# 512-column products in the gate and in the output projection's second half of a two-layer encoder trunk, with their low weights at six offsets

## The chip, the core and the metric

The kernel runs on one core of a Trainium2 chip. Its time is the device time of one execution in microseconds, lower is better; medians are over several executions.

## What is computed

Two layers work on a sequence of 256 positions with 2048 channels, all in float32.

```
h = x
for each layer:
    hn = rmsnorm(h);  u = hn @ w_in            # 5632 columns: conv value, conv gate, z, q, k, v, z2
    ya = swish(layernorm(conv31(value * sigmoid(gate)))) * silu(z)
    yb = window_attention(q, k, v) * silu(z2)
    h  = h + concat(ya, yb) @ w_out            # 2048 x 2048, the output projection
    e  = rmsnorm(p @ w_pe)
    h  = h + e * sigmoid(h @ w_pg)             # 2048 x 2048, the gate
return rmsnorm(h)
```

## The kernel before

Everything is kept transposed: channels on the 128 partitions, the 256 positions along the free dimension. A tile of 128 output channels is a sum over 16 slices of 128 input channels.

**Products.** The products are made in a reduced form of float32 (f32r), three for each slice. Both operands are split into a high part (rounded to f32r) and a low part (the rest): high weights with high operand, high weights with low operand, low weights with high operand. `mm3` (lines 398 to 403) issues these three products of 256 columns, and each brings its own load of 128x128 weights, so the high weights are loaded twice:

```
L401  matmul(o, w[:, 0], x[:, 0], ...)      # high weights, high operand
L402  matmul(o, w[:, 0], x[:, 1], ...)      # high weights, low operand
L403  matmul(o, w[:, 1], x[:, 0], ...)      # low weights, high operand
```

**Weights.** They come as a stream of *halves*: 128x1024 numbers each, 8 slices of one output tile. There are 156 per layer in a fixed order (`weight_halves`), the output projection's first half (the channels of `yb`) at 92 to 107, its second half (those of `ya`) at 108 to 123, the gate at 124 to 155. Two halves are one DMA of 1024 KB from SyncE (`load`). `split` makes a half's high part by a cast on ScalarE (line 168) and its low part by a subtraction on VectorE (line 171). `get` runs the splits four halves ahead of the products; five buffers (`NSPL`) hold split halves, so half n+5 can be cast only when TensorE is done with half n. `SHIFT` places both parts 16 numbers (64 bytes) into their buffer, the low part right behind the high one.

**Order.** The queues of TensorE, VectorE and ScalarE run in the order in which the program writes them (`MAN`). An instruction that waits holds up everything behind it on its engine. After each half `pump` lets side work go on by a step: in the gate the normalised embedding's products (line 540), one instruction per half, and in the projection the low part of the residual of the pair before (line 771).

**Output projection.** First for all 16 tiles the slices of `yb`, then (lines 761 to 775) for all 16 the slices of `ya`: a pair of tiles shares one PSUM bank, one VectorE add of 128x512 puts it on the residual (line 769), a cast on ScalarE makes the residual's high part (line 770), a subtraction its low part (line 771). High and low part of the residual, `h1`, are the gate's operand.

**Gate.** Pairs of tiles again, two halves for each tile. `gate(j, b)` (lines 785 to 811) adds the residual's two parts (line 790), takes the sigmoid of the PSUM bank on ScalarE (line 792), multiplies and adds on VectorE (lines 794, 795) and squares for the next norm on ScalarE (line 391 or 800), with the accumulation on GpSimd. In the last layer two ScalarE copies scale the result for the output (line 808). The last two tiles go one by one. The first pair takes the lower eight slices of both tiles, then the upper eight.

At the border of the layers the sum of squares (`rstd_col`, line 354) needs the square of the gate's last tile.

Of the kernel before, what the change touches and what calls it, by code (L numbers as in the profile page):

```python
# [10 lines left out]
F32 = mybir.dt.float32  # L11
# [6 lines left out]
P = 128  # L18
D = 2048
S = 256  # L20
DEPTH = 2
KT = D // P
# [6 lines left out]
W_KV = NKV * HD  # L29
# [9 lines left out]
HALF = 1024  # L39
# [9 lines left out]

NB_FIRST = KT  # L50
NSPL = 5
SHIFT = 16
MAN = 'DVE,PE,Activation'
LY = (2, 2)
ORD = 1
# [65 lines left out]
NHALF = len(HALVES)  # L121
# [8 lines left out]
def trunk_kernel(ctx: ExitStack, tc: tile.TileContext, xT, pT, wst, par, gain, relb, sinkp, onehot, out):  # L130
    nc = tc.nc
# [7 lines left out]
    wk = ctx.enter_context(tc.tile_pool(name="wk", bufs=2))  # L139
# [7 lines left out]
    def halves(t):  # L147
        return [t[:, 0], t[:, 1]]

    def bank(name):  # L150
        return ps.tile([P, 2, S], F32, tag="ps", name=name)
# [3 lines left out]
    raws, spl = {}, {}  # L155
# [7 lines left out]
    def split(h):  # L163
        raw = raws[h // 2][:, h % 2, :]
        w = wspl.tile([P, 2 * HALF + 64], F32R, tag="w", name=f"w{h}")
        w = w[:, SHIFT:SHIFT + 2 * HALF].rearrange("p (t n) -> p t n", t=2)
        hi, lo = w[:, 0], w[:, 1]
        nc.scalar.copy(hi, raw)  # L168
        spl[h] = w
        if h not in (4, 5):  # L170
            nc.vector.tensor_sub(lo, raw, hi.bitcast(F32))  # L171

    def first_lo(h):

        w = spl[h]
        nc.vector.tensor_sub(w[:, 1], raws[h // 2][:, h % 2, :], w[:, 0].bitcast(F32))

    def ahead(h):

        while state["spl"] < min(h, TOT - 1):  # L180
            n = state["spl"] + 1
            while state["raw"] < min(n // 2 + LD - 1, TOT // 2 - 1):
                state["raw"] += 1
                load(state["raw"])
            if HALVES[n % NHALF][0] != "w_pe" or n >= NHALF:
                split(n)
            state["spl"] = n

    def get(h):

        r = h % NHALF
        if r < 12:
            ahead(h + (r | 1) + 2 - r)
        else:
            ahead(h + LS)
        return spl.pop(h)
# [82 lines left out]
    h = halves(bigt("x"))  # L279
# [118 lines left out]
    def mm3(o, w, x, start, stop):  # L398


        nc.tensor.matmul(o, w[:, 0], x[:, 0], start=start, stop=False, skip_group_check=True)  # L401
        nc.tensor.matmul(o, w[:, 0], x[:, 1], start=False, stop=False, skip_group_check=True)  # L402
        nc.tensor.matmul(o, w[:, 1], x[:, 0], start=False, stop=stop, skip_group_check=True)  # L403

    class Cursor:
        h = 0

    def step(o, X, start, stop):

        steps([o], X, [start], stop)  # L410

    def steps(os, X, starts, stop):

        parts = []
        for _ in os:
            name, _, k0, nk = HALVES[Cursor.h % NHALF]
            parts.append(get(Cursor.h).rearrange("p t (k c) -> p t k c", k=nk))
            Cursor.h += 1
        for kk in range(nk):
            k = k0 + kk  # L420
            for o, w, start in zip(os, parts, starts):
                mm3(o, w[:, :, kk, :], X[k // 8][:, :, k % 8, :], start and kk == 0, stop and kk == nk - 1)
        for _ in os:
            pump()

    def pair(X, name):
        b = bank(name)
        for x in range(2):
            step(b[:, x, :], X, x == 0, False)
            step(b[:, x, :], X, False, True)  # L430
        return b

    def hilo(hi, lo, src):
# [5 lines left out]
    for l in range(DEPTH):  # L439
# [4 lines left out]
        hg = []  # L444
# [27 lines left out]
        for q in range(4):  # L472
            n = Cursor.h
            Cursor.h += 1
            if l:
                w = get(n).rearrange("p t (j k c) -> p t j k c", j=4, k=2)
            else:
                raw = raws[n // 2][:, n % 2, :].rearrange("p (j k c) -> p j k c", j=4, k=2)
            for jj in range(0, 4, 2):
                j = 4 * q + jj  # L480
                b = bank("e")
                for x in range(2):
                    for k in range(2):
                        if l:
                            mm3(b[:, x, :], w[:, :, jj + x, k, :], pp[:, :, k, :], x == 0 and k == 0, k == 1)
                        else:
                            nc.tensor.matmul(b[:, x, :], raw[:, jj + x, k, :], pf[:, k, :], start=x == 0 and k == 0,
                                             stop=k == 1, skip_group_check=True)
                if l == 0 and j // 2 < 4:
                    for k in (4 * (j // 2), 4 * (j // 2) + 2):  # L490
                        if k < KT - 2:
                            square_acc(hacc, h[k // 8][:, k % 8:k % 8 + 2, :], k == 0, nc.vector)
                    if j // 2 == 3:
                        sq = wk.tile([P, 2, S], F32, name="sq", tag="sq", bufs=3)
                        nc.scalar.activation(sq, h[1][:, 6:8, :], AF.Square)
                        hparts = halves_of(sq) + [fold(hacc)]
                if j // 2 == QQ[l][0]:
                    dg = rstd_col(hparts, D, f"rh{l}")
                    ahead(5 if l == 0 else Cursor.h - 1 - q + 5)
                if j // 2 == QQ[l][1]:  # L500
                    rbs.append(rstd_row(dg, f"rh{l}", copy=False))
                    if l == 0:
                        first_lo(4)
                        operands(0, 1)
                        first_lo(5)
                        subs.pop(0)()
                        operands(2, 1)
                if QQ[l][1] + (l == 0) <= j // 2 <= QQ[l][1] + 1:
                    operands(4 * (j // 2 - QQ[l][1]), 2)
                ecopy.append((j, b))  # L510

                while ecopy and 4 * (l == 0) <= j // 2 < 6:
                    copied(*ecopy.pop(0))
            pump()
# [36 lines left out]
        a, zb = halves(az)  # L551
# [26 lines left out]
        for ts in FIRST_TILES:  # L578
            bs = [bank(f"ag{l}_{t}") for t in ts]
# [14 lines left out]
        b = pair(hg, f"k{l}")  # L594
# [8 lines left out]
        vb = [bank(f"v{l}_{b}") for b in range(2)]  # L603
        for q in range(4):
            n = Cursor.h
            Cursor.h += 1
            w = get(n).rearrange("p t (k c) -> p t k c", k=4)
            for kk in range(4):
                k = 4 * q + kk
                for b in range(2):  # L610
                    mm3(vb[b][:, 0, :], hg[k // 8][:, :, k % 8, b * P:(b + 1) * P], w[:, :, kk, :],
                        k == 0, k == KT - 1)
            pump()
        v = wk.tile([P, 2, W_KV], F32, name=f"v{l}", tag="v", bufs=1)
        for b in range(2):
# [59 lines left out]
        for i in range(0, 8, 2):  # L675

            b = pair(hg, f"zb{l}_{i}")
            nc.scalar.activation(zb[:, i:i + 2, :], b, AF.Silu)
            b = pair(hg, f"q{l}_{i}")
# [3 lines left out]
            for hh in range(2):  # L683
                r, o = rows_of[hh], rows_of[1 - hh]
# [7 lines left out]
        for t in range(0, NCT, 2):  # L692
            b = pair(hg, f"za{l}_{t}")
# [55 lines left out]
        Y = [ya, yb]  # L749
        for k in (0, 4):  # L750
            nc.gpsimd.dma_start(zb[:, k:k + 4, :], hsrc[:, 8 + k:12 + k, :])
        h1 = []
        for j in range(0, KT, 2):
            b = bank(f"o{l}_{j}")
            for x in range(2):
                step(b[:, x, :], Y, x == 0, True)
            d = az[:, j // 8, j % 8:j % 8 + 2, :]
# [3 lines left out]
        for j in range(0, KT, 2):  # L761
            d = az[:, j // 8, j % 8:j % 8 + 2, :]
            if j % 8 == 0:
                h1.append(bigt(f"h1{l}_{j // 8}", F32R))
            hi, lo = (x[:, j % 8:j % 8 + 2, :] for x in halves(h1[-1]))
            b = bank(f"o{l}_{j}")
            for x in range(2):
                step(b[:, x, :], Y, x == 0, True)
            nc.vector.tensor_add(d, b, d)
            nc.scalar.copy(hi, d)  # L770
            sub = lambda d=d, hi=hi, lo=lo: nc.vector.tensor_sub(lo, d, hi.bitcast(F32))
            if j < KT - 2:
                later(sub)
            else:
                sub()
# [3 lines left out]
        last = l == DEPTH - 1  # L779
# [36 lines left out]
        hparts = []  # L816
        for j in range(0, KT - 2, 2):
            if j:
                b = pair(h1, f"g{l}_{j}")
            else:  # L820
                b = bank(f"g{l}_{j}")
                for n in range(2):
                    for x in range(2):
                        step(b[:, x, :], h1, n == 0 and x == 0, n == 1)
            gate(j, b)
            if j == 4 and not last:
                pp = wk.tile([P, 4 * S + 32], F32R, name="pp", tag="qq")
                pp = pp[:, 24:24 + 4 * S].rearrange("p (x k s) -> p x k s", x=2, k=2)
                hilo(pp[:, 0], pp[:, 1], pf)
        for j in range(KT - 2, KT):  # L830
            b = bank(f"g{l}_{j}")[:, 0:1, :]
            for n in range(2):
                step(b[:, 0, :], h1, n == 0, n == 1)
            gate(j, b)
        drain()
        h = e

# [7 lines left out]
    for j in (0, 2, 12, 4, 6, 14, 8, 10):  # L845
        for x in [slice(0, 1), slice(1, 2)] if j == 0 else [slice(0, 2)]:
            d = og[j // 8][:, j % 8:j % 8 + 2, :][:, x, :]
# [82 lines left out]
```

## Time and profile before

| | |
|---|---|
| median of 3 runs | 942.38 us (942.35 to 943.13) |
| the profiled execution | 943.05 us |
| its span, first to last instruction | 941.3 us |
| mean granted TensorE clock | 0.996 |
| TensorE busy | 928.9 us (99%) |
| VectorE busy | 767.9 us (82%) |
| ScalarE busy | 550.3 us (58%) |
| output projection, second half, layer 0 | 340.3 to 383.8 us |
| gate, layer 0 | 383.8 to 470.9 us |
| output projection, second half, layer 1 | 797.2 to 840.7 us |
| gate, layer 1 | 840.7 to 928.0 us |

In the rows of the profile PE is TensorE's products, PEld its weight loads, DVE VectorE, ACT ScalarE, POOL GpSimd, SP SyncE. A row of the timeline has the start, the time, the engine, the line of the program, the operation, what it writes and reads, their shapes and a count; in square brackets how long the engine sat idle before it and what ended that. Where a row merges several instructions (xN), its time is from the first one's start to the last one's end. A row of windows has, for a stretch, each engine's busy time and instructions, the granted TensorE clock, the DMA engines' share and their GB/s. A matmul's duration includes its way through the array, so the distance between starts, not the duration, tells what one costs.

### The profile page before, as it was taken

What the parts mean: (1) busy time and instruction counts of PE and PEld (TensorE: products, weight loads), DVE (VectorE), ACT (ScalarE), POOL (GpSimd) and SP (SyncE); (2) the same over time, 40 slices, a digit from 0 to 9 for tenths busy, and PEclk for the clock granted to TensorE, in tenths of its full rate; (3) what the DMA queues carried; (4) which work ended last, traced back from release to release, by engine and by line L of the source; (5) the groups of instructions that cost most, each with busy time, mean ns of one, the idle gap of its engine ahead of it and who ended that gap; (6) DMA issues with size and microseconds to landing.
All of it is one profiled execution on the core that took longest, in us unless ns stands there. A gap on an engine that the chain in (4) does not pass through costs nothing.

```text
span 941.3 us, 19132 instructions
## 1 busy us (share of the span) xinstructions
PE 928.9 (99%) x7968; PEld 912.3 (97%) x7968; DVE 767.9 (82%) x1290; ACT 550.3 (58%) x830; POOL 83.0 (9%) x79
## 2 busy tenths in 40 slices
PE   8999999999999999999999999999999999999995
PEld 7999999999999999999999999999999999999995
DVE  3999999998787786786679999999887877777663
ACT  4655455787874555554467445568778546445551
POOL 0023001010000000011102100000100000000111
PEclk9999999999999999999999999999999999999999
DMA  8674556555546456556545556566455554655532
GB/s 296 230 253 162 197 180 237 191 202 186 171 158 249 156 213 211 189 180 232 212 183 205 183 198 222 179 213 201 170 169 180 176 206 146 257 179 180 198 117 90
DMA packets 29011, 182.55 MB, mean 194 GB/s; under 512 B 3595, under 2 KB 4156, under 8 KB 9084
## 3 DMA queue, kind: packets, MB, share of 16 engines
q1 hardware_dynamic: 24284, 165.70, 49.7%
q0 software_dynamic: 3344, 12.88, 4.2%
q10 hardware_dynamic: 1296, 2.75, 0.8%
q8 instruction: 62, 1.02, 0.4%
q14 instruction: 25, 0.20, 0.1%
HBM read 177.09 MB, written 4.23 MB: 193 GB/s over the span
## 4 chain that ended last, share of the span: by engine, by line
PE 95%; DVE 2%; DMA 1%; ACT 1%; issue 0%; ACTq 0%; DVEq 0%
PE o L401 6%; PE o L402 6%; PE o L403 6%; PE ag L401 6%; PE g L403 6%; PE ag L403 6%; PE ag L402 6%; PE g L402 6%; PE g L401 6%; PE za L401 3%; PE za L403 3%; PE za L402 3%; PE zb L401 3%; PE zb L403 3%; PE zb L402 3%; PE q L401 3%
## 5 line engine op out<-in xcount | busy, mean ns | idle before, releaser
L171 DVE TENSOR_TENSOR w<-raw,w 128x1024 fp32r<-128x1024 f32 x306 | 374.4, 1232 | 101.4 <-ACT w L168 100.4
L168 ACT CAST w<-raw 128x1024 fp32r<-128x1024 f32 x308 | 316.2, 1046 | 156.6 <-PE ag L403 44.0
L565 DVE SCALAR_TENSOR_TENSOR cz<-az,pars,cz 128x241 f32<-128x241 f32 (+11 forms) x480 | 216.2, 500 | 1.0
L401 PE MATMUL ag<-hg,w 128*128 128x256 f32 x512 | 141.9, 277 | 0.0
L403 PE MATMUL g<-h,w 128*128 128x256 f32 x512 | 141.5, 276 | 0.0
L402 PE MATMUL ag<-hg,w 128*128 128x256 f32 x512 | 141.5, 276 | 0.0
L403 PE MATMUL ag<-hg,w 128*128 128x256 f32 x512 | 141.5, 276 | 0.0
L401 PE MATMUL g<-h,w 128*128 128x256 f32 x512 | 141.4, 276 | 0.0
L402 PE MATMUL g<-h,w 128*128 128x256 f32 x512 | 141.4, 276 | 0.0
L401 PEld LDWEIGHTS ag<-hg,w 128*128 128x128 f32 x512 | 96.1, 188 | 0.9 <-ACT w L168 0.8
L402 PEld LDWEIGHTS ag<-hg,w 128*128 128x128 f32 x512 | 96.2, 188 | 0.0
L402 PEld LDWEIGHTS g<-h,w 128*128 128x128 f32 x512 | 96.1, 188 | 0.0
L403 PEld LDWEIGHTS ag<-hg,w 128*128 128x128 f32 x512 | 96.1, 188 | 0.0
L401 PEld LDWEIGHTS g<-h,w 128*128 128x128 f32 x512 | 96.1, 188 | 0.0
L403 PEld LDWEIGHTS g<-h,w 128*128 128x128 f32 x512 | 96.1, 188 | 0.0
L401 PE MATMUL za<-hg,w 128*128 128x256 f32 x256 | 71.9, 281 | 0.0
L401 PE MATMUL q<-hg,w 128*128 128x256 f32 x256 | 71.9, 281 | 0.0
L401 PE MATMUL o<-yb,w 128*128 128x256 f32 x256 | 71.9, 281 | 0.0
L401 PE MATMUL zb<-hg,w 128*128 128x256 f32 x256 | 71.5, 279 | 0.0
L402 PE MATMUL q<-hg,w 128*128 128x256 f32 x256 | 71.4, 279 | 0.0
L403 PE MATMUL q<-hg,w 128*128 128x256 f32 x256 | 71.4, 279 | 0.0
L402 PE MATMUL o<-yb,w 128*128 128x256 f32 x256 | 71.3, 278 | 0.0
(227 smaller groups left out, 2273.0 us busy)
## 6 DMA issues: line engine op xcount, KB each, us to landing
raw<-in_wst SPq DMA_DIRECT2D x153, 1024.0 KB, 4.9
bias<-fscr POOLq DMA_DIRECT2D x16, 384.0 KB, 3.9
raw<-in_wst SPq DMA_DIRECT2D x4, 512.0 KB, 7.9
az<-in_xT POOLq DMA_DIRECT2D x4, 512.0 KB, 5.6
hscr<-e POOLq DMA_DIRECT2D x2, 1024.0 KB, 5.6
az<-hscr POOLq DMA_DIRECT2D x4, 512.0 KB, 5.4
x<-in_xT SPq DMA_DIRECT2D x3, 512.0 KB, 8.2
out_t<-og ACTq DMA_DIRECT2D x4, 256.0 KB, 3.0
```

The source lines that it names most:

```text
L168: nc.scalar.copy(hi, raw)
L171: nc.vector.tensor_sub(lo, raw, hi.bitcast(F32))
L401: nc.tensor.matmul(o, w[:, 0], x[:, 0], start=start, stop=False, skip_group_check=True)
L402: nc.tensor.matmul(o, w[:, 0], x[:, 1], start=False, stop=False, skip_group_check=True)
L403: nc.tensor.matmul(o, w[:, 1], x[:, 0], start=False, stop=stop, skip_group_check=True)
L565: nc.vector.scalar_tensor_tensor(acc[:, t, lo_:hi_], a[:, t, lo_ + s:hi_ + s], w(k), acc[:, t, lo_:hi_], ALU.mult, ALU.add)
```

## The change

In the output projection's second half and in the gate (but for the last tile of the last layer) `mm3` gets a whole PSUM bank for one tile: one product of the high weights with the operand's high and low part side by side (512 columns, the result's two halves kept apart in the bank), then the low weights with the high operand into the second half of the bank. Two weight loads instead of three, the same number of columns. The two halves of a bank are added afterwards: in the projection by two VectorE adds of 128x256 per tile into the residual; in the gate by `merge`, a ScalarE copy of one half to a tile in SBUF and a VectorE add of the other, per tile; the sigmoid then reads this SBUF tile.

The buffers of the split weights are laid out anew: the high part stays 64 bytes into its buffer, the low part starts 1056 numbers in (before: 1040) plus an offset, which differs in six stretches: 64, 96 and 0 bytes in layer 0 (projection's second half, first and second half of the gate), 32, 16 and 80 bytes in layer 1; 64 bytes for all other halves.

```
-SHIFT = 16
+SHIFT = (64, 64)
+SHIFTS = [
+    [(108, 64, 64), (124, 64, 96), (140, 64, 0)],
+    [(108, 64, 32), (124, 64, 16), (140, 64, 80)],
+]
+def shift(h):
+    for k, a, b in SHIFTS[h // NHALF]:
+        if k <= h % NHALF < k + 16:
+            return a // 4, b // 4
+    return SHIFT[0] // 4, SHIFT[1] // 4
...
     def split(h):
-        w = w[:, SHIFT:SHIFT + 2 * HALF].rearrange("p (t n) -> p t n", t=2)
-        hi, lo = w[:, 0], w[:, 1]
+        a, b = shift(h)
+        hi, lo = w[:, a:a + HALF], w[:, HALF + 32 + b:2 * HALF + 32 + b]
...
     def mm3(o, w, x, start, stop):
-        nc.tensor.matmul(o, w[:, 0], x[:, 0], start=start, stop=False, ...)
-        nc.tensor.matmul(o, w[:, 0], x[:, 1], start=False, stop=False, ...)
-        nc.tensor.matmul(o, w[:, 1], x[:, 0], start=False, stop=stop, ...)
+        if len(o.shape) == 3:
+            nc.tensor.matmul(o, w[0], x, start=start, stop=False, ...)
+            nc.tensor.matmul(o[:, 1], w[1], x[:, 0], start=False, stop=stop, ...)
+            return
+        prod3(o, w, parts_of(x), start, stop)       # the three products as before
+
+    def merge(bs):
+        t = wk.tile([P, 2, S], F32, name="hl", tag="ptt")[:, 0:len(bs), :]
+        for x, b in enumerate(bs):
+            nc.scalar.copy(t[:, x, :], b[:, 1, :])
+            nc.vector.tensor_add(t[:, x, :], b[:, 0, :], t[:, x, :])
+        return t
+
+    def wide(X, name):
+        b = bank(name)
+        step(b, X, True, False)
+        step(b, X, False, True)
+        return b
...
         # output projection, second half
-            b = bank(f"o{l}_{j}")
             for x in range(2):
-                step(b[:, x, :], Y, x == 0, True)
-            nc.vector.tensor_add(d, b, d)
+                b = bank(f"o{l}_{j + x}")
+                step(b, Y, True, True)
+                for y in range(2):
+                    nc.vector.tensor_add(d[:, x, :], b[:, y, :], d[:, x, :])
             nc.scalar.copy(hi, d)
...
         # gate
             if j:
-                b = pair(h1, f"g{l}_{j}")
+                bs = [wide(h1, f"g{l}_{j + x}") for x in range(2)]
             else:
-                b = bank(f"g{l}_{j}")
+                bs = [bank(f"g{l}_{x}") for x in range(2)]
                 for n in range(2):
-                    for x in range(2):
-                        step(b[:, x, :], h1, n == 0 and x == 0, n == 1)
-            gate(j, b)
+                    for b in bs:
+                        step(b, h1, n == 0, n == 1)
+            gate(j, merge(bs))
...
         for j in range(KT - 2, KT):
-            b = bank(f"g{l}_{j}")[:, 0:1, :]
-            for n in range(2):
-                step(b[:, 0, :], h1, n == 0, n == 1)
-            gate(j, b)
+            if last and j == KT - 1:
+                ...                                 # as before
+            else:
+                gate(j, merge([wide(h1, f"g{l}_{j}")]))
```

More of the change, by code (lines that the diff above doesn't have):

```diff
@@ L165, in split @@
         w = wspl.tile([P, 2 * HALF + 64], F32R, tag="w", name=f"w{h}")
-        w = w[:, SHIFT:SHIFT + 2 * HALF].rearrange("p (t n) -> p t n", t=2)
-        hi, lo = w[:, 0], w[:, 1]
+        a, b = shift(h)
+        hi, lo = w[:, a:a + HALF], w[:, HALF + 32 + b:2 * HALF + 32 + b]
         nc.scalar.copy(hi, raw)
-        spl[h] = w
+        spl[h] = (hi, lo)
         if h not in (4, 5):
@@ L173, in first_lo @@
     def first_lo(h):
-        w = spl[h]
-        nc.vector.tensor_sub(w[:, 1], raws[h // 2][:, h % 2, :], w[:, 0].bitcast(F32))
+        hi, lo = spl[h]
+        nc.vector.tensor_sub(lo, raws[h // 2][:, h % 2, :], hi.bitcast(F32))
     def ahead(h):
@@ L398, in mm3, with prod3, parts_of @@
     def mm3(o, w, x, start, stop):
-        nc.tensor.matmul(o, w[:, 0], x[:, 0], start=start, stop=False, skip_group_check=True)
-        nc.tensor.matmul(o, w[:, 0], x[:, 1], start=False, stop=False, skip_group_check=True)
-        nc.tensor.matmul(o, w[:, 1], x[:, 0], start=False, stop=stop, skip_group_check=True)
+        if len(o.shape) == 3:
+            nc.tensor.matmul(o, w[0], x, start=start, stop=False, skip_group_check=True)
+            nc.tensor.matmul(o[:, 1], w[1], x[:, 0], start=False, stop=stop, skip_group_check=True)
+            return
+        prod3(o, w, parts_of(x), start, stop)
+    def prod3(o, w, x, start, stop):
+        nc.tensor.matmul(o, w[0], x[0], start=start, stop=False, skip_group_check=True)
+        nc.tensor.matmul(o, w[0], x[1], start=False, stop=False, skip_group_check=True)
+        nc.tensor.matmul(o, w[1], x[0], start=False, stop=stop, skip_group_check=True)
+    def parts_of(x):
+        return [x[:, 0], x[:, 1]]
+    def merge(bs):
[4 more added lines that the diff above has]
+        return t
     class Cursor:
@@ L416, in steps @@
             name, _, k0, nk = HALVES[Cursor.h % NHALF]
-            parts.append(get(Cursor.h).rearrange("p t (k c) -> p t k c", k=nk))
+            parts.append(get(Cursor.h))
             Cursor.h += 1
@@ L421, in steps @@
             for o, w, start in zip(os, parts, starts):
-                mm3(o, w[:, :, kk, :], X[k // 8][:, :, k % 8, :], start and kk == 0, stop and kk == nk - 1)
+                mm3(o, [y[:, kk * P:(kk + 1) * P] for y in w], X[k // 8][:, :, k % 8, :],
+                    start and kk == 0, stop and kk == nk - 1)
         for _ in os:
@@ L475, in trunk_kernel @@
             if l:
-                w = get(n).rearrange("p t (j k c) -> p t j k c", j=4, k=2)
+                w = [y.rearrange("p (j k c) -> p j k c", j=4, k=2) for y in get(n)]
             else:
@@ L484, in trunk_kernel @@
                         if l:
-                            mm3(b[:, x, :], w[:, :, jj + x, k, :], pp[:, :, k, :], x == 0 and k == 0, k == 1)
+                            mm3(b[:, x, :], [y[:, jj + x, k, :] for y in w], pp[:, :, k, :], x == 0 and k == 0, k == 1)
                         else:
@@ L606, in trunk_kernel @@
             Cursor.h += 1
-            w = get(n).rearrange("p t (k c) -> p t k c", k=4)
+            w = get(n)
             for kk in range(4):
@@ L610, in trunk_kernel @@
                 for b in range(2):
-                    mm3(vb[b][:, 0, :], hg[k // 8][:, :, k % 8, b * P:(b + 1) * P], w[:, :, kk, :],
-                        k == 0, k == KT - 1)
+                    prod3(vb[b][:, 0, :], parts_of(hg[k // 8][:, :, k % 8, b * P:(b + 1) * P]),
+                          [y[:, kk * W_KV:(kk + 1) * W_KV] for y in w], k == 0, k == KT - 1)
             pump()
@@ L830, in trunk_kernel @@
         for j in range(KT - 2, KT):
-            b = bank(f"g{l}_{j}")[:, 0:1, :]
-            for n in range(2):
-                step(b[:, 0, :], h1, n == 0, n == 1)
-            gate(j, b)
+            if last and j == KT - 1:
+                b = bank(f"g{l}_{j}")[:, 0:1, :]
+                for n in range(2):
+                    step(b[:, 0, :], h1, n == 0, n == 1)
+                gate(j, b)
+            else:
+                gate(j, merge([wide(h1, f"g{l}_{j}")]))
         drain()
```

## The prediction

> **What bounds the kernel now.** I read the page first: the engines' shares, the clock and the chain that ended last.
>
> ```profile
> span 941.3 us, 19132 instructions
> ...
> PE 928.9 (99%) x7968; PEld 912.3 (97%) x7968; DVE 767.9 (82%) x1290; ACT 550.3 (58%) x830; POOL 83.0 (9%) x79
> ...
> PE 95%; DVE 2%; DMA 1%; ACT 1%; issue 0%; ACTq 0%; DVEq 0%
> ```
>
> TensorE is never idle and makes 95% of the chain; VectorE at 82% is the next to run out. Then the three stages that the change touches, as windows: the output projection's second half and the gate of layer 0, the gate of layer 1.
>
> ```profile
> core 0: us, PE busy (x) PEld busy (x) DVE busy (x) ACT busy (x) POOL busy (x), PEclk, DMA share, GB/s
> 340.30:383.80 43.50, 43.50 (x386) 43.50 (x385) 31.51 (x35) 21.13 (x24) 0.00 (x0) 1.00 0.62 218
> 383.80:470.90 87.10, 87.10 (x771) 87.10 (x770) 63.81 (x78) 43.68 (x51) 8.39 (x7) 1.00 0.58 206
> ...
> 840.70:928.00 87.30, 87.30 (x773) 87.30 (x772) 57.04 (x74) 45.26 (x61) 7.76 (x6) 1.00 0.41 145
> ```
>
> 43.5 us hold 16 weight halves of 24 products, 87.1 us hold 32: 2.72 us a half, 113.4 ns a product, 340 ns for the three products of one 128-row slice. DMA has room (0.4 to 0.6).
>
> **What a product costs.** TensorE streams and loads weights side by side, so I looked for rows in which only one of the two can set the pace.
>
> ```profile
> 17.72 1.70 PEld L487 LDWEIGHTS e<-p,raw 128*128 128x128 f32 x8
> ...
> 927.67 0.53 PEld L354 LDWEIGHTS rfc<-ones,fold 128*128 128x128 f32 x4
> 928.12 1.20 PEld L347 LDWEIGHTS idle<-ident,ones 128*128 128x128 f32 x10
> ...
> 245.17 0.19 PEld L633 LDWEIGHTS sc<-keys1h,qq 128*128 128x128 f32 x1
> ...
> 246.00 0.19 PEld L633 LDWEIGHTS sc<-keys1l,qq 128*128 128x128 f32 x1
> ```
>
> With one column to stream (L354) loads follow at (0.53-0.19)/3 = 113 ns, with 128 columns (L347) at (1.20-0.19)/9 = 112 ns: a load alone sets 112 to 113 ns, so the present 113.4 ns is load-bound. Where a pass streams longer (L487, plain f32) each load hides and passes follow at (1.70-0.19)/7 = 216 ns. The new high product streams twice 256 columns behind one load; I take 216 ns for it, from the row that is nearest in length, and 113.3 for the low one, during which the next high load must land: 329.3 ns a slice against 340. Other end: if a load costs the stream its excess over pure streaming (113.3-106.7, half of the 213.3 taken for a long pass) at every load, it is 213.3+106.7+2x6.7 = 333.3. The score products (L633, same 256 columns) follow at (246.00-245.17)/7 = 119 ns; at that excess, 12 ns a load, it would be 344. So 329 to 344, and 325 if both loads vanish into 2.5 ns each (216-213.3).
>
> The Trainium skill, "TensorE: Matmul & The Clock Gate", section "Back-to-back issue gap", gives N/2.4 + 2.5 ns warm: 109.2 for 256 columns, 215.8 for 512. The trace has 113.4 for the first, so the rule misses here; by it a slice would take 325 ns and TensorE alone would gain 11.3 us.
>
> Changed slices: 16 halves per layer in the projection, 32 and 30 in the gates, 94 halves of 8. TensorE alone: 752 x 10.7 ns = **8.0 us** (4.1 in layer 0, 3.9 in layer 1); ends 11.3 us gained, 3.0 us lost. The lows' distances cost nothing in instructions; if they matter, it is inside these ends.
>
> **What it adds elsewhere.** A projection pair had one 512-wide PSUM add; it now has four 256-wide ones. A gate pair gets two ScalarE copies and two VectorE adds of 256, and its sigmoid waits for them. No DMA is moved, and no queue order but VectorE's and ScalarE's. These two queues run in written order, so what counts is their loop, not their busy share. In the first two pairs of layer 0:
>
> ```profile
> 343.64 0.69 DVE L758 TENSOR_TENSOR az<-o,az 128x512 f32<-128x512 f32 x1
> 344.24 2.35 DVE L171 TENSOR_TENSOR w<-raw,w 128x1024 fp32r<-128x1024 f32 x2
> 346.51 0.69 DVE L769 TENSOR_TENSOR az<-o,az 128x512 f32<-128x512 f32 x1
> 348.83 1.23 DVE L171 TENSOR_TENSOR w<-raw,w 128x1024 fp32r<-128x1024 f32 x1 [1.64 <-ACT w L168]
> 349.97 0.69 DVE L771 TENSOR_TENSOR h<-az,h 128x512 fp32r<-128x512 f32 x1
> 350.58 1.22 DVE L171 TENSOR_TENSOR w<-raw,w 128x1024 fp32r<-128x1024 f32 x1
> 351.71 0.68 DVE L769 TENSOR_TENSOR az<-o,az 128x512 f32<-128x512 f32 x1
> ...
> 347.23 0.62 ACT L770 CAST h<-az 128x512 fp32r<-128x512 f32 x1 [2.94 <-DVE az L769]
> 347.75 2.03 ACT L168 CAST w<-raw 128x1024 fp32r<-128x1024 f32 x2
> ...
> 466.62 0.41 DVE L790 TENSOR_TENSOR hs<-h 128x256 f32<-128x256 f32 x1
> 466.96 0.41 DVE L794 TENSOR_TENSOR e<-e,sg 128x256 f32<-128x256 f32 x1
> 467.40 0.42 DVE L795 TENSOR_TENSOR e<-e,hs 128x256 f32<-128x256 f32 x1
> ```
>
> The pair's loop is add, high copy of the residual (ScalarE), cast of the next weights behind it, its subtraction, the residual's low part, the second subtraction, add: 346.51 to 351.71, 5.20 us against TensorE's 5.44. The cover is 0.24 us. A 256-wide op takes 0.44 us to one that needs it (466.96 to 467.40) and 0.34 to one that doesn't (466.62 to 466.96); I take 0.45 and 0.35. The two adds of a tile go into the same place. The new loop, from a pair's last add: 0.45 to the high copy, 0.52 to the cast, 1.08 to the subtraction, 1.14 to the low part, 0.61 to the first tile's adds, 0.45 + 0.35 for them, 1.14 for the second subtraction, 0.45 between the last adds: **6.19 us** against TensorE's new 5.27. The look-ahead of four halves hides that until it is used up.
>
> The first pair's last add: 344.24 + 1.14 + 0.45 + 0.35 + 1.14 + 0.45 = 347.77; the eighth's, 7 x 6.19 later, 391.1. Its high copy ends at 392.2, its low part at 392.9. TensorE meets these two rows in the gate's third half, seventh slice. The present gate starts at 383.83:
>
> ```profile
> 383.83 0.28 PE L401 MATMUL g<-h,w 128*128 128x256 f32 x1
> ```
>
> so the stage starts at 383.83 - 16 x 2.72 = 340.3, and TensorE would be there at 340.3 + 18 x 2.634 + 6 x 0.329 = 389.7. **It waits 3.2 us, once in each layer.** The start of layer 1's stage looks alike (the same add at 800.54):
>
> ```profile
> 800.54 0.68 DVE L758 TENSOR_TENSOR az<-o,az 128x512 f32<-128x512 f32 x1
> ```
>
> Gate of layer 1, the present loop:
>
> ```profile
> 862.70 0.60 ACT L792 ACTIVATE sg<-g 128x512 f32<-128x512 f32 x1 [1.61 <-PE g L403]
> 864.78 0.63 ACT L391 ACTIVATE sq<-e 128x512 f32<-128x512 f32 x1 [1.48 <-DVE e L795]
> 865.32 0.89 ACT L808 ACTIVATE og<-e,gains 128x256 f32<-128x256 f32 x2
> 866.12 3.12 ACT L168 CAST w<-raw 128x1024 fp32r<-128x1024 f32 x3
> ...
> 867.19 1.23 DVE L171 TENSOR_TENSOR w<-raw,w 128x1024 fp32r<-128x1024 f32 x1 [2.44 <-ACT w L168]
> ...
> 873.54 0.69 DVE L790 TENSOR_TENSOR hs<-h 128x512 f32<-128x512 f32 x1
> ...
> 932.23 0.37 ACT L851 COPY rfrb<-rf2b 128x256 f32<-128x256 f32 x1 [1.98 <-PE rf2b L368]
> ```
>
> Sigmoid to subtraction 4.49, four subtractions with the embedding's products 6.35: 10.84 of TensorE's 10.88. The merge puts a copy (0.37, L851) and an add ahead of the sigmoid, 0.85 us, and 0.35 more on VectorE for the tile that is ready earlier: about 11.5 (0.5 less what the loop now waits for TensorE's slots) against 10.54, for the three pairs in which those products last. The two buffers left after the stall cover part; following the steps I get 1.6 us of waits. Layer 0 has no L808 pair (0.80 us): about 10.7, which the look-ahead takes. At the layer's border the square of the last tile has 2 us in hand:
>
> ```profile
> 472.89 0.42 ACT L800 ACTIVATE sq<-e 128x256 f32<-128x256 f32 x1 [1.09 <-DVE e L795]
> ...
> 475.29 0.53 PEld L354 LDWEIGHTS rh1c<-ones,sq 128*128 128x128 f32 x4
> ```
>
> TensorE comes 0.9 us earlier and the square some 1.2 later behind the longer queue: 0.2 us of wait. The kernel's last tile keeps its form, so the tail is as it was.
>
> Sum: layer 0 -4.1 + 3.2 + 0.2 = -0.7; layer 1 -3.9 + 3.2 + 1.6 = +0.9. Together **+0.2 us** on the profiled execution's own 943.05 (span 941.3): 943.2. The median shown, 942.38, is 0.7 lower. A slower product (333.3) gives +1.3, since the waits shrink as TensorE slows: what VectorE and ScalarE allow sets the end, whatever a product costs. Under 0.2% (1.9 us) a measurement can't tell from no change.
>
> **Rivals.**
> Faster: the adds into one place overlap like independent ones (0.34 us, 466.62 to 466.96), or the queues hide more than I count. The wait is gone once the loop is 5.73 us or less (40.1 us for seven periods, from 347.77 to 387.9); four intervals at 0.34 instead of 0.45 bring it to 5.75. Then TensorE's 8.0 us come through: 935. Against: the dependent interval stands in each such pair.
>
> The clock drops in the new wait. The trace has one such case:
>
> ```profile
> 16.39 1.05 PE L354 MATMUL rh0c<-ones,sq 128*128 128x1 f32 x8 [1.15 <-ACT sq L495]
> ...
> 18.00:20.00 2.00, 2.00 (x9) 1.42 (x9) 1.23 (x2) 2.00 (x4) 1.63 (x1) 0.79 1.01 382
> 20.00:21.00 1.00, 1.00 (x5) 0.91 (x5) 0.39 (x1) 1.00 (x4) 0.00 (x0) 0.50 0.48 197
> 21.00:22.00 1.00, 1.00 (x3) 0.80 (x3) 1.00 (x3) 0.95 (x2) 0.00 (x0) 0.50 0.08 16
> 22.00:23.00 1.00, 1.00 (x5) 0.78 (x4) 1.00 (x2) 0.13 (x1) 0.00 (x0) 0.72 0.00 0
> ```
>
> After 1.15 us idle and one-column products for another 1.4, the granted clock is 0.50 for (1-0.79)x2/0.5 + 2 + 0.28x1/0.5 = 3.4 us. A wait of 3.2 us can do the same: 1.7 us lost, in layer 1 mostly regained from its later waits. One window: 944.9; two and some: 946.6. The same page of the Trainium skill, Part 1, "What's actually happening", has the clock fall only after a whole idle window of about 3.4 us, by which this rival costs nothing; the row above, with 1.15 us wholly idle, speaks against taking that literally.
>
> Slower by the products: long f32r streams collide with loads as the scores do, 344 ns or a little more in some of the six stretches. TensorE then loses 3.0 us and still meets part of the waits (it arrives at 392.0, so 0.9 a layer): 943.05 + 3.0 + 1.8 = 947.9.
>
> **Chances.** Forecast 0.43, faster rival 0.19, clock 0.24, colliding products 0.14. The clock's case lies on the bound, half in "same". Faster 0.21, same 0.48, slower 0.31. The range reaches down to 935.0 and up to 947.9; the likeliest case's own is 941.9 to 944.9.
>
> **What will show it.** Timeline of TensorE: 512-wide products at 216 to 220 ns and low ones at 113. In the projection's second half VectorE without gaps but those for the cast, and pairs of adds 6.2 us apart. In the gate's third half one TensorE wait of 2.5 to 3.5 us for the residual's low part (line of the subtraction from VectorE), in layer 1 shorter ones for weights. Granted clock 0.50 there, or not. Wrong would be: no waits of TensorE and a gain, a loop near 5.3, or products over 340 ns a slice.

## The result, and the profile after

The changed kernel takes 948.01 us (median of 4 executions, 946.78 to 948.44) against 942.37 before: ratio 1.0053, interval 1.0041 to 1.0065. It is 5.6 us slower. The forecast was 943.2 with no measurable change. The total is that of the third rival (947.9), but it came about in another way than that rival said.

The profiled execution took 946.78 us. Its mean granted clock is 0.998, that of the three others 0.994 to 0.995: the stretch at half clock near 20 us, which the profile before had, is missing in it. The first products behind that stretch start 1.4 us earlier than before (23.32 against 24.72 us), so this execution lies below the median.

The page of the changed kernel: span, busy time, chain.

```profile
span 945.0 us, 17736 instructions
...
PE 932.5 (99%) x7216; PEld 882.4 (93%) x7216; DVE 790.9 (84%) x1369; ACT 556.2 (59%) x861; POOL 82.0 (9%) x79
...
PE 92%; DVE 5%; ACT 1%; DMA 1%; issue 1%; POOL 0%; ACTq 0%; DVEq 0%
```

752 products and loads fewer, and TensorE is busy 3.6 us longer. Windows of the changed kernel over the touched stages, cut where the offset changes (columns as before: length, then busy time and instructions of each engine, clock, DMA):

```profile
337.81:383.02 45.21, 45.21 (x258) 39.55 (x257) 34.62 (x53) 18.08 (x22) 0.00 (x0) 1.00 0.55 188
383.02:427.97 44.95, 44.95 (x258) 39.40 (x257) 37.90 (x55) 25.92 (x35) 2.58 (x2) 1.00 0.53 186
427.97:473.20 45.23, 45.23 (x259) 39.60 (x257) 33.03 (x43) 23.77 (x34) 5.80 (x5) 1.00 0.64 228
...
797.58:842.81 45.23, 45.23 (x259) 39.05 (x257) 34.63 (x53) 18.10 (x22) 0.00 (x0) 1.00 0.54 187
842.81:886.33 43.52, 43.52 (x259) 38.49 (x257) 33.66 (x51) 25.59 (x38) 2.59 (x2) 1.00 0.56 193
```

Each stretch is 16 halves of 8 slices: 45.21 us is 353 ns a slice, 44.95 is 351, 43.52 is 340. TensorE waits in none of them and the clock is 1.00. Five of the six stretches (the last, from 886.33, goes at 353 ns too) are slower than the 340 ns of the three 256-column products before. The sixth, with the low weights at 16 bytes, is exactly as fast.

The time between the first products of the stages, in the profiled executions (the gate of layer 1 up to TensorE's last product):

| stage | before | changed | all at 16 bytes | new layout, old products | 16 bytes, later cast |
|---|---|---|---|---|---|
| projection 2nd half, layer 0 | 43.52 | 45.21 | 43.52 | 43.52 | 43.52 |
| gate, layer 0 | 87.04 | 90.17 | 91.02 | 87.04 | 87.04 |
| projection 2nd half, layer 1 | 43.52 | 45.23 | 43.52 | 43.52 | 43.52 |
| gate, layer 1 | 91.18 | 92.87 | 95.22 | 91.18 | 91.39 |
| z2 and q, layer 0 | 103.37 | 102.61 | 102.63 | 102.68 | 102.63 |
| z2 and q, layer 1 | 103.88 | 102.42 | 102.45 | 102.43 | 102.41 |

The four touched stages cost 8.2 us. The untouched ones give back 3.1 us on balance: 2.2 in z2 and q, 2.0 in z and in the projection's first half, less 1.2 that the stages ahead of z2 lose. Their products are as before, only the low weights lie 128 bytes further from the high ones. With the 1.4 us of the clock that makes the 3.7 us between the two profiled executions.

### The profile page after: what moved, and what is told of

It is laid out like the page before. It is cut to its first block, busy times and chain, and to the rows that moved or that the text cites. A ratio compares the mean times of both kernels' runs of the same rounds, so it can differ in the third digit from the quotient of the medians.

```text
span 945.0 us, 17736 instructions
## 1 busy us (share of the span) xinstructions
PE 932.5 (99%) x7216; PEld 882.4 (93%) x7216; DVE 790.9 (84%) x1369; ACT 556.2 (59%) x861; POOL 82.0 (9%) x79
## 4 chain that ended last, share of the span: by engine, by line
PE 92%; DVE 5%; ACT 1%; DMA 1%; issue 1%; POOL 0%; ACTq 0%; DVEq 0%
PE g L414 12%; PE o L414 6%; PE g L415 6%; PE ag L423 6%; PE ag L421 6%; PE ag L422 6%; PE o L415 3%; PE za L421 3%; PE o L421 3%; PE o L423 3%; PE o L422 3%; PE za L423 3%; PE za L422 3%; PE zb L423 2%; PE q L423 2%; PE zb L421 2%
## 5 line engine op out<-in xcount | busy, mean ns | idle before, releaser
L180 ACT CAST w<-raw 128x1024 fp32r<-128x1024 f32 x308 | 312.1, 1045 | 119.2 <-PE ag L423 44.1
L414 PE MATMUL g<-h,w 128*128 128x512 f32 x496 | 173.3, 393 | 0.0
L415 PE MATMUL g<-h,w 128*128 128x256 f32 x496 | 138.9, 280 | 0.0
L414 PEld LDWEIGHTS g<-h,w 128*128 128x128 f32 x496 | 92.9, 187 | 21.4
L415 PEld LDWEIGHTS g<-h,w 128*128 128x128 f32 x496 | 93.3, 188 | 0.0
L414 PE MATMUL o<-ya,w 128*128 128x512 f32 x256 | 90.5, 397 | 0.0
L415 PE MATMUL o<-ya,w 128*128 128x256 f32 x256 | 71.9, 281 | 0.0
L421 PE MATMUL o<-yb,w 128*128 128x256 f32 x256 | 71.5, 279 | 0.0
L421 PE MATMUL q<-hg,w 128*128 128x256 f32 x256 | 71.2, 278 | 0.0
L421 PE MATMUL zb<-hg,w 128*128 128x256 f32 x256 | 71.1, 278 | 0.0
L422 PE MATMUL o<-yb,w 128*128 128x256 f32 x256 | 70.9, 277 | 0.0
L423 PE MATMUL o<-yb,w 128*128 128x256 f32 x256 | 70.8, 276 | 0.0
L423 PE MATMUL zb<-hg,w 128*128 128x256 f32 x256 | 70.8, 276 | 0.0
```

The costliest lines, as they stand in the source:

```text
L414: nc.tensor.matmul(o, w[0], x, start=start, stop=False, skip_group_check=True)
L415: nc.tensor.matmul(o[:, 1], w[1], x[:, 0], start=False, stop=stop, skip_group_check=True)
L421: nc.tensor.matmul(o, w[0], x[0], start=start, stop=False, skip_group_check=True)
L422: nc.tensor.matmul(o, w[0], x[1], start=False, stop=False, skip_group_check=True)
L423: nc.tensor.matmul(o, w[1], x[0], start=False, stop=stop, skip_group_check=True)
```

## The experiments

Theory after the result: a slice costs what its streamed columns cost, and the offset of the low weights decides whether that is 340 or about 353 ns; the number of loads is no matter. Rival: the loop of VectorE and ScalarE, 6.2 us a pair of tiles. Second rival: phase alone, that is, how the products happen to fall in time, with no part for the offset.

**The low weights at 16 bytes in all six stretches.**

```
-    [(108, 64, 64), (124, 64, 96), (140, 64, 0)],   and layer 1
+SHIFTS = [[(108, 64, 16), (124, 64, 16), (140, 64, 16)]] * 2
```

> The changed kernel with the low weights at 16 bytes in all six stretches (in the changed kernel only the first half of layer 1's gate has 16; it alone took 340 ns a slice, the others 350 to 353). If the offset decides: 340 ns in all six, TensorE as fast as before and no faster, so that the loop of VectorE and ScalarE (6.2 us a pair) shows as waits in the gate's third half, 1.5 to 2.3 us a layer: stages together 3.5 us over before instead of 8.2, time 943.3. If it is a chance of phase and not the offset: slices of 353 ns stay in several stretches, time 946 to 949.

Measured 946.18 us, ratio 1.0032 (1.0019 to 1.0044): not the 943.3 of the offset theory but in the range given for phase (946 to 949). Both projection stages are at 340 ns a slice, as the offset theory has it. Then the loop shows. Timeline of this kernel around the gate's third half, TensorE and VectorE (start, time, engine):

```profile
389.36 0.28 PE L412 MATMUL g<-h,w 128*128 128x256 f32 x1
391.00 0.51 PE L411 MATMUL g<-h,w 128*128 128x512 f32 x1 [1.37 <-DVE h L808]
...
388.69 0.88 DVE L806 TENSOR_TENSOR az<-o,az 128x256 f32<-128x256 f32 x2
390.25 0.69 DVE L808 TENSOR_TENSOR h<-az,h 128x512 fp32r<-128x512 f32 x1 [0.68 <-ACT h L807]
```

TensorE waits for the residual's last low part; the next product is due at 389.36 + 0.11 and starts at 391.00: 1.53 us. The wait is where the forecast had it, and layer 1 has the same one. Windows of the same kernel before, around and after it:

```profile
338.47:381.99 43.52, 43.52 (x258) 38.49 (x257) 33.27 (x51) 17.83 (x21) 0.00 (x0) 1.00 0.55 194
...
391.81:473.01 81.20, 81.20 (x466) 71.04 (x465) 64.72 (x87) 44.93 (x64) 8.40 (x7) 1.00 0.59 211
...
389.00:391.00 2.00, 0.63 (x4) 0.30 (x3) 1.28 (x4) 1.40 (x2) 0.00 (x0) 1.00 0.60 119
391.00:393.00 2.00, 2.00 (x11) 1.77 (x12) 2.00 (x4) 2.00 (x4) 0.00 (x0) 1.00 0.92 389
```

The clock stays at 1.00 through it. But behind the wait 29 halves take 81.20 us, 350 ns a slice, at the same offset that gave 340 ahead of it. So the offset alone doesn't decide; a break in TensorE's stream can move it from one pace into another, and it stays there. Only one execution was profiled; the six of this kernel lie between 944.43 and 947.45 us, so the pace behind the wait may not be the same in each.

**The new layout with the old products**, bank use and adds (offset 64 everywhere).

```
-SHIFTS = [[(108, 64, 64), ...], [...]]
+SHIFTS = [[], []]
 # projection and gate: step(b[:, x, :], ...), one add per pair, pair(h1, ...) as before
```

> The layout of the changed kernel (low weights 1056 numbers plus 64 bytes into the buffer, everywhere) with the three 256-column products, bank use and adds of the kernel before. If the 512-column form with its offsets carries the whole loss: the four stages at 340 ns a slice as before, no waits, and the gain that the changed kernel has in its untouched stages stays: 948.0 - 8.2 = 939.8. If the layout itself slows products: stages over 43.5 and 87.1 us, time 942 or more.

Measured 939.46 us, ratio 0.9959 (0.9945 to 0.9973): the forecast of 939.8 holds. The whole loss of the changed kernel hangs on the 512-column form with its offsets, and the layout by itself gains 0.4%. Windows over z2 and q in layer 1, this kernel's row and then before's:

```profile
592.59:695.02 102.43, 102.32 (x890) 99.50 (x889) 95.36 (x204) 75.38 (x134) 10.42 (x11) 1.00 0.60 204
```

```profile
592.87:696.75 103.88, 103.88 (x890) 101.25 (x889) 95.75 (x205) 75.44 (x134) 10.37 (x11) 1.00 0.59 202
```

The same 890 products take 1.45 us less: of the distances between starts, 443 are near 118 ns before and 33 here, nearly all others near 113.

**A sweep of the offset**, a new one every third half.

```
+    k = h % NHALF - 108
+    if k >= 0:
+        return 16, k // 3 + 16 * (h // NHALF)      # in steps of 4 bytes
```

> The changed kernel with a new offset every third half of the changed stages: 0 to 60 bytes in steps of 4 in layer 0, 64 to 124 in layer 1. If the offset decides the pace: the slice's time is a function of it, 340 at 16, 353 at 0, 32, 64 and 80, 351 at 96, perhaps lower somewhere; under 329 would mean that the forecast of 329.3 was right for a good offset. If phase decides: the values at these six offsets do not come back.

**The same sweep with three 256-column products.**

> The three 256-column products with a new offset every third half of the projection's second half and of the gate, as in the sweep of the 512-column form. If each form has its own good offsets: 340 ns at 64, 353 at 16, and the two sweeps disagree at most offsets. If the offset acts alike on both: the same list, against the runs with 16 bytes throughout.

ns per slice (distance between high products' starts, mean of a stretch):

| offset, bytes | 0 | 4 | 16 | 28 | 32 | 40 | 52 | 64 | 76 | 80 | 96 | 100 | 112 | 116 |
|---|---|---|---|---|---|---|---|---|---|---|---|---|---|---|
| 512 + 256 columns | 350 | 340 | 340 | 340 | 353 | 351 | 347 | 353 | 344 | 347 | 351 | 340 | 341 | 340 |
| 3 x 256 columns | 355 | 353 | 353 | 356 | 353 | 340 | 340 | 340 | 340 | 353 | 353 | 353 | 353 | 353 |

The 17 offsets left out lie between 347 and 353 in the first row (not counting the slices at two waits of TensorE) and between 350 and 359 in the second. No offset is below 340, let alone at 329. The good offsets of the two forms hardly overlap. Four of the six offsets of the changed kernel come back (16, 32, 64, 96); 0 and 80 have 350 and 347 here and 353 there. Each offset was run once, in one order, and the pace depends on what went before: at 88 bytes the slices took 347 to 360 ns ahead of a wait and 340 behind it. So the rows are no list that holds elsewhere.

**What the parts of a slice cost.** Products are shortened or left out, so the result is incomplete.

```
+            m = 0 if start else PROBE[...]     # by stretches of 8 halves
+            if m >= 0:  wide product
+            if m:       low product of abs(m) columns
```

> Leaves out part of the products of the changed stages, after each tile's first slice, in stretches of 8 halves; low weights at 16 bytes. Layer 0: complete; wide product alone (two stretches); wide and 64, 128, 192 columns of the low product. Layer 1: low product alone with 256, 128, 64 columns; wide alone; wide and 128; complete. My forecast's theory, a load takes 112 ns and a longer stream hides it: wide alone 216, low alone 113 at 256, 128 and 64 columns alike, wide and 128 columns 216 + 112. Rival, the stream itself takes 17 cycles for 16 columns whatever is loaded: wide alone 226.7, low alone with 256 columns 113.3, and only with 128 and 64 columns does the load show (112). Second rival, a load costs the stream 6.7 ns: wide alone 220.

Timeline rows of wide products alone, of wide products with 64 low columns, and with 192:

```profile
369.75 1.56 PE L414 MATMUL o<-ya,w 128*128 128x512 f32 x6
...
409.89 0.19 PE L416 MATMUL g<-h,w 128*128 128x64 f32 x1
409.92 0.48 PE L414 MATMUL g<-h,w 128*128 128x512 f32 x1
410.24 0.19 PE L416 MATMUL g<-h,w 128*128 128x64 f32 x1
...
456.80 0.25 PE L416 MATMUL g<-h,w 128*128 128x192 f32 x1
456.89 0.41 PE L414 MATMUL g<-h,w 128*128 128x512 f32 x1
457.14 0.25 PE L416 MATMUL g<-h,w 128*128 128x192 f32 x1
```

Alone, wide products follow at (1.56 - 0.39)/5 = 234 ns: neither my 216 nor the 220 of a fixed price per load, and above the 227 (medians) of the complete slices with 16 bytes throughout. A slice with 64 low columns takes 350 ns in these rows (409.89 to 410.24) and 348 as the median of its stretch, one with 128 takes 347, one with 192 takes 340: leaving out more columns bought nothing. A load's 112 ns from the low product's start and 235 for the wide one give 347, so the load price of the forecast fits, and a low product of 64 or 128 columns can't hide it. (It is not the same everywhere: in the next run low products follow at 108 to 109 ns with a load each.) Slices with all 256 low columns go at 349 to 350 ns in this kernel, also at 16 bytes, where the run with 16 bytes throughout had 340; each tile's first slice lacks its low product here, and that break may be the reason. In layer 1, TensorE waited so much for split weights that the clock fell to 0.50 from 806 to 864 us. There low products of 128 and of 64 columns both follow at 213 ns, so it isn't the columns that set this time; it fits the load, 107 ns at full clock by this.

**The streamed operand as one column repeated** (stride 0), in either product, both or none; where it is repeated the result is not that of the program.

```
+            x2 = x[:, :, 0:1].broadcast_to([P, 2, S])
+            wide product from x2 or x, low product from x2[:, 0] or x[:, 0]
```

> 512-column form at 16 bytes; in stretches of 8 halves the streamed operand is one column repeated (stride 0) instead of 256 different ones, so part of the result is left wrong: layer 0: none, both products, both, wide alone, low alone, none; layer 1: wide, low, none, both, wide, low. If the stream is slowed by fetching its operand from SBUF (17 cycles for 16 columns of 64 bytes): wide 215 to 216 and low 109 to 112 where the column is repeated. If it is a pace of the array or of the loads: 226.7 and 113.3 everywhere.

Rows of one kernel: none repeated, both, the wide one alone, the low one alone.

```profile
343.14 0.39 PE L414 MATMUL o<-ya,w 128*128 128x512 f32 x1
343.37 0.28 PE L415 MATMUL o<-ya,w 128*128 128x256 f32 x1
343.49 0.39 PE L414 MATMUL o<-ya,w 128*128 128x512 f32 x1
...
365.05 0.38 PE L414 MATMUL o<-ya,w 128*128 128x512 f32 x1
365.27 0.27 PE L415 MATMUL o<-ya,w 128*128 128x256 f32 x1
365.38 0.38 PE L414 MATMUL o<-ya,w 128*128 128x512 f32 x1
...
412.00 0.38 PE L414 MATMUL g<-h,w 128*128 128x512 f32 x1
412.22 0.28 PE L415 MATMUL g<-h,w 128*128 128x256 f32 x1
412.34 0.38 PE L414 MATMUL g<-h,w 128*128 128x512 f32 x1
...
435.15 0.39 PE L414 MATMUL g<-h,w 128*128 128x512 f32 x1
435.39 0.27 PE L415 MATMUL g<-h,w 128*128 128x256 f32 x1
435.50 0.39 PE L414 MATMUL g<-h,w 128*128 128x512 f32 x1
```

Medians of the stretches: none 227 + 113 ns in the first, 232 to 235 + 117 (a slice of 350) in the two others. Both: 218.5 + 109, a slice of 327.5. Wide alone: 215 + 118. Low alone: 232 + 108. With the same loads and the same number of columns, a wide product that streams one column repeated takes 215 to 218.5 ns and a low one 108 to 109; next to it a product of different columns stays at 232 or 118. So the columns that are streamed set the price, not the loads, and 329 ns, the slice of the forecast, is reached only with repeated ones. A repeated column changes the addresses and the data at once; that the addresses do it is likely from the sweeps, but not shown apart.

This kernel also shows what the forecast's pace would have brought. At 327.5 ns TensorE comes to the residual's last low part 2.6 us early (due at 388.31, started at 390.90), and then the clock falls. Its rows and the windows behind the wait:

```profile
388.20 0.27 PE L415 MATMUL g<-h,w 128*128 128x256 f32 x1
390.90 0.79 PE L414 MATMUL g<-h,w 128*128 128x512 f32 x1 [2.43 <-DVE h L811]
...
390.00:391.00 1.00, 0.10 (x1) 0.10 (x1) 0.84 (x2) 1.00 (x3) 0.00 (x0) 0.87 0.66 213
391.00:392.00 1.00, 1.00 (x3) 0.91 (x4) 1.00 (x3) 1.00 (x3) 0.00 (x0) 0.50 0.96 401
...
394.00:395.00 1.00, 1.00 (x7) 0.89 (x6) 1.00 (x3) 0.18 (x1) 0.00 (x0) 0.92 0.00 0
```

From 391 to 394 all three windows have 0.50, so the clock is at half for (1 - 0.87) x 2 + 3 + (1 - 0.92) x 2 = 3.4 us, and 1.7 us of TensorE's work is lost. In layer 1, where the wait is 1.7 us, it stays at 1.00.

**512 columns in the gate alone, at 16 bytes.**

> The changed kernel with all low weights at 16 bytes and only the gate in the 512-column form; the projection's second half has its three 256-column products and its one add per pair again. Loop theory (the wait in the gate's third half comes from the projection's 6.2 us loop, and the wait throws the products into a slower phase): no wait, the gate stays at 340 ns a slice, gate stages 87.1 us, time as the layout alone, 939.5. Rival (the gate's own longer way to the sigmoid makes the wait, or 512-column products of the gate slow down anyway): gate stages 3 to 4 us longer, time 946.

Measured 947.78 us, ratio 1.0055 (1.004 to 1.007): a miss, and one of my edit. It left the projection's 256-column products at 16 bytes, a bad offset for them. Windows over the projection's second half and the gate in layer 0:

```profile
338.69:383.91 45.22, 45.22 (x386) 45.22 (x385) 31.74 (x35) 21.05 (x24) 0.00 (x0) 1.00 0.59 210
383.91:473.52 89.61, 89.61 (x515) 78.34 (x513) 67.55 (x91) 47.89 (x66) 8.39 (x7) 1.00 0.56 197
```

353 ns a slice in the projection; the gate enters at that pace and stays at 350, without any wait of TensorE. With the projection at 64 bytes:

```
-SHIFTS = [[(108, 64, 16), (124, 64, 16), (140, 64, 16)]] * 2
+SHIFTS = [[(108, 64, 64), (124, 64, 16), (140, 64, 16)]] * 2
```

> As the run with the 512-column gate at 16 bytes and the 256-column projection, but the projection's second half at 64 bytes, the offset at which 256-column products ran at 340 ns a slice. If only the offset was wrong there (16 bytes is good for the 512-column form alone): projection's second half back at 43.5 us, gate at 340 ns, no waits, 939 to 940. If the gate by itself costs: gate stages over 87.5 and 91.5 us, over 943.

939.17 us, ratio 0.9958 (0.9941 to 0.9974), as expected; 43.52 us and 87.04 us, no waits. The gate's merge costs nothing. In layer 1 the gate takes 0.2 us more than before; that is its last tile, whose 48 products of 256 columns have their low weights at 16 bytes too and follow at 117.9 ns.

**256-column products at 16 bytes everywhere.**

```
-SHIFT = (64, 64)
+SHIFT = (64, 16)
```

> Three 256-column products everywhere as in the kernel before, low weights 1056 numbers plus 16 bytes in. If the offset decides how often narrow products fall into the slow pace: at 16 as at 64 bytes fewer slow halves than before (from 117.8 to 113.3 ns a product), 938.5 to 940. If the 128 bytes more between high and low weights do it by themselves, the offset being of no weight: the same as with 64 bytes, 939.5. If 64 was luck: back at 942.

970.69 us, ratio 1.0297 (1.0281 to 1.0312): far outside every expectation. Windows over the two stages of layer 0:

```profile
348.69:393.92 45.23, 45.23 (x387) 45.23 (x386) 30.92 (x34) 20.45 (x23) 0.00 (x0) 1.00 0.59 210
393.92:484.37 90.45, 90.45 (x771) 90.45 (x770) 64.22 (x77) 43.64 (x51) 8.39 (x7) 1.00 0.56 198
```

Nearly all products go at 117.8 ns. 48 bytes in the place of the low weights are worth 31 us here, more than the whole change.

**512 columns in the projection alone, at 16 bytes**, with its loop; the gate with 256 columns at 64 bytes.

> Only the projection's second half in the 512-column form, at 16 bytes and with the loop of 6.2 us; the gate with 256-column products at 64 bytes. Loop theory: one wait of 1.5 us in the gate's third half of each layer, 939.5 + 3.1 = 942.6; more only if the wait throws the 256-column products into the 353 ns pace behind it (up to 3 us a layer, 948). Rival (the wait belongs to the gate's merge): no wait, 939.5.

942.37 us, ratio 0.9993 (0.9984 to 1.0003), where the loop theory had 942.6. TensorE in the gate's third half:

```profile
389.60 0.28 PE L420 MATMUL g<-h,w 128*128 128x256 f32 x1
390.51 0.39 PE L418 MATMUL g<-h,w 128*128 128x256 f32 x1 [0.64 <-ACT h L807]
391.24 0.38 PE L419 MATMUL g<-h,w 128*128 128x256 f32 x1 [0.34 <-DVE h L808]
```

It waits for the high part and again for the low part; each gate is 1.57 us longer than before. The wait belongs to the projection's loop. Behind it the products go on at 113.4 ns, as before: a wait does not always change the pace.

**The loop shortened**: the residual's high cast goes behind the next weight cast, all low weights at 16 bytes.

```
-            nc.scalar.copy(hi, d)
-                later(sub)
+                later(lambda d=d, hi=hi, sub=sub: (nc.scalar.copy(hi, d), later(sub)))
```

> Both stages in the 512-column form at 16 bytes; the cast of the residual's high part is put behind the next weight cast on ScalarE, its low part one half later, so that the weight cast no longer waits for the adds. Loop theory: the loop falls from 6.2 us to VectorE's own work (two weight subtractions, four adds, one low part: 2 x 1.14 + 4 x 0.4 + 0.6 = 4.5), below TensorE's 5.44; no wait, 340 ns throughout, 939.5. Rival (the adds alone are too much for VectorE): the wait of 1.5 us in the gate's third half stays, time 944 to 946.

938.80 us, ratio 0.9957 (0.9943 to 0.9972). VectorE in the projection:

```profile
352.34 0.89 DVE L806 TENSOR_TENSOR az<-o,az 128x256 f32<-128x256 f32 x2 [0.37 <-PE o L412]
...
357.78 0.88 DVE L806 TENSOR_TENSOR az<-o,az 128x256 f32<-128x256 f32 x2 [0.37 <-PE o L412]
```

The pairs are 5.44 us apart, TensorE's own pace, and the adds wait for TensorE. All stages are at 340 ns, but for the same last tile in layer 1's gate (0.2 us). This beats both kernels, but by the layout's gain alone: with the old products the layout gives 939.46 (ratios 0.9957 and 0.9959).

**The same edit in the changed kernel, with its six offsets.**

> The changed kernel with its own six offsets, and only the residual's high cast moved behind the next weight cast, which shortens the projection's loop. If the offsets alone make the loss, and the loop is hidden because the products are slow: no change against the changed kernel, 948.0. If the loop takes part: 944 or less.

946.19 us, ratio 1.0033 (1.0022 to 1.0044): between the two expectations, 948.0 and 944. The stages up to the gate of layer 1 are the same to 0.01 us in the profile, without waits in either kernel; what differs is the last stretch, offset 80, which goes at 347 ns a slice here instead of 353 (0.7 us). That is a pace, as the sweep had it for 80 bytes, and no wait of the loop. So the loop takes no part in the changed kernel's loss. The rest of the 1.8 us between the two medians fits the stretch at half clock near 20 us: by their mean granted clocks, three of the changed kernel's four executions have it (0.994 and 0.995) and only one of these seven clearly does (0.995, 947.56 us). Without it the two profiled executions differ by 0.94 us, 946.78 and 945.84.

## Why the prediction was right or wrong

The forecast's likeliest case failed, and that the time lies next to the third rival's is luck. By its own steps:

*The product's price: wrong, and the step that failed.* The 216 ns came from plain float32 passes, taken as the nearest row in length. Those passes stream 256 columns in 216 ns, 0.84 ns a column; f32r takes 113.3 ns for 256, 0.44 a column, and at that rate 512 columns cost 226.7. Measured were 227 at best (16 bytes throughout) and 231 to 236 elsewhere (the changed kernel, wide products alone). The 113.4 ns of a 256-column product I read as load-bound, with 112 ns for a load beside it. Both prices are real and lie 1.5 ns apart (a load can even take less: 108 to 109 ns with repeated columns), so taking a load away leaves the stream as the bound. A slice measured 340 to 353 against my 329.3. The Trainium skill's N/2.4 + 2.5 ns ("TensorE: Matmul & The Clock Gate", "Back-to-back issue gap") is met within 3 ns with a repeated column (218.5 and 109) and missed with real operands (227 and 113).

*The offsets: mis-sized.* I put them inside 329 to 344. The low weights' place moves a slice between 340 and 353, which is 8.2 us over the touched stages, and 31 us where all products follow. I also put the new layout at nothing outside these stages; it gives back 3.1 us there. The third rival had slower products as the cause, but as a collision with loads, which no run shows, at 344 ns, 3.0 us in all, and with waits of 0.9 us a layer. What came was 8.2 us, no waits, and 3.1 us back, with nearly the same total.

*The loop of VectorE and ScalarE: right.* 6.19 us a pair was the sum; the changed kernel's timeline shows it.

```profile
342.84 0.87 DVE L809 TENSOR_TENSOR az<-o,az 128x256 f32<-128x256 f32 x2
...
349.01 0.87 DVE L809 TENSOR_TENSOR az<-o,az 128x256 f32<-128x256 f32 x2
...
386.10 0.88 DVE L809 TENSOR_TENSOR az<-o,az 128x256 f32<-128x256 f32 x2
...
389.59 0.69 DVE L811 TENSOR_TENSOR h<-az,h 128x512 fp32r<-128x512 f32 x1 [0.69 <-ACT h L810]
```

342.84 to 349.01 is 6.17; seven periods to 386.10 are 6.18 each. The last low part ends 52.5 us after the stage's start (forecast 52.6).

*The wait: right in place and cause, hidden in the changed kernel by the slower products.* TensorE's rows in the same kernel, seventh slice of the gate's third half:

```profile
390.63 0.28 PE L415 MATMUL g<-h,w 128*128 128x256 f32 x1
390.75 0.40 PE L414 MATMUL g<-h,w 128*128 128x512 f32 x1
```

It gets there at 390.75, 0.47 us after the low part is done. With 340 ns a slice the forecast's step gives 52.6 - (18 x 2.72 + 6 x 0.34) = 1.6 us; 1.53 and 1.57 were measured. At 327.5 ns in most of the way there, the repeated columns had a wait of 2.6 us.

*The gate's loop in layer 1: not seen.* 1.6 us of waits were forecast for 329 ns a slice; at 340 there are none. No run has that loop at 329 ns, so the term is not tested at the forecast's pace.

*The clock rival: not in the changed kernel, but right where the wait comes.* The changed kernel has no wait there. A wait of 1.5 us between dense products leaves the clock at 1.00; one of 2.6 us, with repeated columns, was followed by 3.4 us at 0.50, the 1.7 us lost that the rival had. At the forecast's own pace this rival, and not the forecast, would likely have come.

*"Whatever a product costs, the loop sets the end": wrong.* At 340 ns the loop still makes TensorE wait; at 353 TensorE sets the end again, and there the offsets had put it. The end also moves with the pace that the products have behind the wait, 340 or 350 ns.

## What to carry to other kernels

Before a load is taken away, ask what the stream alone costs, from a row with the same number format; two bounds that lie 1% apart hide each other. A shorter TensorE time must also be matched by the queues that free its operands: write down their loop and compare it with the new pace. Where f32r products run back to back, try where the weights lie in their buffer before anything else is changed: here it was worth more than the change.

## What was not expected of the hardware

The pace of back-to-back f32r products depends on the byte offset between high and low weights: 113.3 ns for 256 columns at 64 bytes, 117.8 at 16, in a kernel that is otherwise the same (939.46 and 970.69 us); the 512-column form has other good offsets. The pace also keeps a state: 340 ns a slice ahead of a wait of 1.5 us and 350 behind it, over 29 halves, with the offset unchanged. The streamed operand takes part in it (repeated column: 327.5 ns a slice). The high weights stayed at 64 bytes in every run, so the low weights' own place and their distance from the high ones are not told apart. Which addresses meet, and why a break shifts the pace, was not settled.
